# One bias table instead of 128 copies, four product banks, and the compression's small networks as steps of their own, in a two-layer attention trunk

## The chip, the cores and the metric

The kernel runs on one core of a Trainium2 chip. The metric is the time of one execution on the device, in microseconds (us); lower is better. Engines are named as the profile names them: PE multiplies matrices (PEld loads its stationary operand), DVE is VectorE, ACT is ScalarE, POOL is GpSimd, and SP issues DMAs.

## What is computed

A trunk of two layers over 256 tokens of width 1024, float32 in and out. The part of the reference that the change touches, cut:

```python
for i in range(DEPTH):                                # 2
    h = h + 0.5 * swiglu(rms_norm(h, g[i, 0]), ffn1_wi[i], ffn1_wo[i])
    n = rms_norm(h, g[i, 1])
    ... = split_cols(n @ w_in[i], IN_SPLITS)
    ya = diff_attention(..., bias_a)                  # 4 heads
    yb = nsa_attention(..., bias_b, cmp_pos, cmp_w1, cmp_w2)   # 8 heads, 2 groups
    yc = swa_sink_attention(..., bias_c)              # 8 heads, window 128
    h = h + (sig(ga) * (ya @ w_br[0]) + sig(gb) * (yb @ w_br[1]) + sig(gc) * (yc @ w_br[2])) @ w_out[i]
    h = h + 0.5 * swiglu(...)                         # second ffn
    h = h + sigmoid(rms_norm(h, g[i, 3]) @ w_ple_gate[i]) * (p[i] @ w_ple[i])
# a head's bias depends on the distance alone: table[rel_bucket(qpos - kpos)]
# in nsa_attention, beside attention over all keys (twice):
k_cmp = gelu(blocks(kc) @ w1[0]) @ w2[0]              # 15 compressed keys, also v_cmp
p_c = masked_softmax(q k_cmp + bias(dist_c));  o_c = p_c @ v_cmp
```

## The kernel before

**Products.** Every large product (`product`, L290) has the activations as stationary operand (128 tokens by 128 features) and 512 weight columns as moving operand, for two token tiles `t`. Float32 is carried as two parts, so that each step `k` is three matmuls (`mul3`, L219: L220, L221, L222). Token tile 1 runs `skew` steps behind tile 0. The result of each tile takes a PSUM bank of the tag `mm`, of which there are two (`mm_bank`, L191). Two more banks have the tag `s` (attention scores), three `tp` (transposes) and one `y`.

**Weights.** `load` (L257) brings 512 KB at a time into one of four `raw` buffers through SP's queue; ACT (L213) and DVE (L208) split it into `wh` and `wl`, in six buffers each. `fetch` keeps three pieces ahead of the use, in the order of the stream. A compile-time planner with a timing model orders each engine's instructions; each engine's queue then runs in that order.

**Feed-forward.** `ffn` (L437) runs 11 products `ff` of 256 gate and 256 up columns, evacuated by ACT L458 (`act`) and DVE L459 (`gated`), turned by DMA transposes on SP's queue (L427), and then two products `fo`.

**Bias.** In the first feed-forward of layer 0, `setup` (L1041) runs in four pieces, after products 4, 5 and 8 and between the two `fo` products. It makes a table of 20 heads by 384 distances (`tb`), writes it to DRAM (`table`, L1061) and from there 128 times into a second DRAM tensor, `rev` (L1062). `rev_band` (L1033) reads a tile `band` of four heads from `rev`, each partition from an address one element lower than the one above it, so that column and partition give the distance. Two bands are read in `setup` on POOL's queue (for `cbias`, L1086 and L1087), ten later on SP's queue.

**Attention.** `attention` (L488) runs the projections A0, A1, A2, Ck, Cq, Bk, Bv, Bq, the three `branch` parts (a gate product and a `br` product for each half of the columns) and the two `wo` products. Between the steps `k` of a product, `Flow.tick` (L162) advances one generator, the side: `attend_a` (L581) from Ck on, `attend_c` (L864) from Bv on, `attend_b` (L793) from `compress` on, at 0.75, 0.6 and 0.7 steps per tick. `flow.join` runs what is left of a side at one place: of A after Bk (L962), of C after branch 0 (L969), of B within branch 1 (L941). The bias is added by DVE L529, which also takes the minimum.

**Compression.** `compress` (L685) runs 64 matmuls `cmp` of 256 columns and then, in one piece, the rest of the two small networks: `c_sb` (L709), eight matmuls `gl` (L712), the gelu on ACT and DVE, `hid`, the matmuls `kc` (L726) and `vc` (L738). `attend_cmp` (L761) computes the scores `sc` against the compressed keys, their softmax `pc` for eight heads of 16 columns, and turns it by eight transposes `pct` (L787) per token tile, one for each head, into 16-row operands `pcT` [16, 2, 512]. `second` (L827) multiplies them with `vc` (16 rows) at L843, as the last part of `yb`. It calls `attend_cmp` before the first use of each token tile, and until `kc` is there it waits with empty steps.

Of the kernel before, what the change touches and what calls it, by code (L numbers as in the profile page):

```python
# [33 lines left out]
PACE_A, PACE_B, PACE_C = 0.75, 0.7, 0.6  # L34
# [101 lines left out]
def _constants():  # L136
    u = np.arange(REV)
    dist = 255 - u
# [10 lines left out]
    return {"onehot": onehot, "dead": dead, "cmask": cmask, "ident": np.eye(128, dtype=np.float32),  # L149
# [3 lines left out]
class Flow:  # L153


    def __init__(self):
        self.side, self.pace, self.due = None, 0.0, 0.0

    def start(self, side, pace):
        self.side, self.pace, self.due = side, pace, 0.0  # L160

    def tick(self):  # L162
        if self.side is not None:
            self.due += self.pace
            while self.due >= 1.0:
                self.due -= 1.0
                if next(self.side, self) is self:
                    self.side = None
                    return

    def join(self):
        if self.side is not None:
            for _ in self.side:
                pass
            self.side = None
# [3 lines left out]
def trunk(ctx: ExitStack, tc: tile.TileContext, a: dict, out: bass.AP, index: list):  # L179
# [11 lines left out]
    def mm_bank(name):  # L191
        return bank("mm", 2, name)

# [294 lines left out]
    def attention(i, norm, after):  # L488
# [3 lines left out]
        def begin():  # L492
            nonlocal pool
            pool = phase("attn")
            for t in range(NT):
                merged[t] = pool.tile([128, D], F32, name=f"merged{t}")
# [58 lines left out]
        def band(first):  # L555
            b = pool.tile([128, 4, 256], F32, tag="band", bufs=2, name="band")
            rev_band(b, first)
# [23 lines left out]
        def attend_a():  # L581
            bnd = band(0)

            def first(u):
# [6 lines left out]
                for st in softmax([p[:, j, :nk] for j in range(4)], [s[j // 2][:, j % 2, :nk] for j in range(4)],  # L591
                                  [bnd[:, 2 * m + j % 2, 256 - nk:] for j in range(4)]):
# [90 lines left out]
        kc, vc = [None], [None]  # L683

        def compress():  # L685
# [22 lines left out]
            c_sb = stage()  # L708
            nc.vector.tensor_copy(c_sb[:64], c_ps[:64])  # L709
            g_ps = tp_bank("gl")[:, :128]  # L710
            for k in range(4):
                nc.tensor.matmul(g_ps[:, 32 * k:32 * k + 32], c_sb[:64, 128 * k:128 * k + 128], fold, start=True, stop=True)  # L712
# [6 lines left out]
            nc.vector.tensor_tensor(gl, gl, g_ps, op=ALU.mult)  # L719
            hid = pool.tile([128, 2, 128], F32R, name="hid")  # L720
            split(hid[:, 0], hid[:, 1], gl)
            w2h, w2l = w2(0)
# [10 lines left out]
            split(kt[:, 0], kt[:, 1], kbd)  # L733
            v_ps = tp_bank("vc")
            for g in range(2):
                for f in range(2):
                    s, n = slice(256 + 64 * f, 320 + 64 * f), slice(64 + 32 * f + 16 * g, 80 + 32 * f + 16 * g)
                    mul3(v_ps[:16, 64 * g:64 * g + 64], hid[:, 0, n], hid[:, 1, n], w2h[:, s], w2l[:, s], f == 0, f == 1)  # L738
            vc[0] = pool.tile([16, 2, 128], F32R, name="vc")
            values(vc[0], v_ps[:16, :128], None)  # L740
# [20 lines left out]
        def attend_cmp(t):  # L761
# [20 lines left out]
            for g in range(2):  # L782
                ps = tp_bank("pct")
                for par in range(2):
                    for m in range(2):
                        j = 2 * par + m
                        nc.tensor.transpose(ps[:16, 128 * j:128 * j + 128], p[:, 4 * g + 2 * m + par, :], ident)  # L787
                T = pool.tile([16, 2, 512], F32R, tag="pcT", bufs=2, name="pcT")
                split(T[:, 0], T[:, 1], ps[:16])
                pcT[t, g] = T  # L790
                yield

        def attend_b():  # L793
# [33 lines left out]
            def second(u, p):  # L827
                g, t, ss = u
                if yB[t] is None:
                    while kc[0] is None:  # L830
                        yield
# [340 lines left out]
```

## Time and profile before

| | us |
|---|---|
| median of 3 runs | 1372.09 |
| lowest, highest | 1371.64, 1373.06 |
| profiled execution | 1372.78 |
| its span, first to last instruction | 1371.0 |

The profiled execution takes 1.78 us more than its span (what lies before the first and after the last instruction), and 0.69 us more than the median. Its trace has a record of each instruction on each engine, of DMA packets, and of the share of PE's clock that was granted (1.00 is 2.4 GHz, 0.50 is 1.2 GHz). In a row `x8` is a count; in square brackets or after a bar stands the time the engine was idle before the instruction, and what ended that idle time.

### The profile page before, as it was taken

What the parts mean: (1) busy time and instruction counts of PE and PEld (TensorE: products, weight loads), DVE (VectorE), ACT (ScalarE), POOL (GpSimd) and SP (SyncE); (2) the same over time, 40 slices, a digit from 0 to 9 for tenths busy, and PEclk for the clock granted to TensorE, in tenths of its full rate; (3) what the DMA queues carried; (4) which work ended last, traced back from release to release, by engine and by line L of the source; (5) the groups of instructions that cost most, each with busy time, mean ns of one, the idle gap of its engine ahead of it and who ended that gap; (6) DMA issues with size and microseconds to landing.
All of it is one profiled execution on the core that took longest, in us unless ns stands there. A gap on an engine that the chain in (4) does not pass through costs nothing.

```text
span 1371.0 us, 18293 instructions
## 1 busy us (share of the span) xinstructions
PE 1341.5 (98%) x6454; PEld 1098.2 (80%) x6454; DVE 944.7 (69%) x1779; ACT 779.4 (57%) x1378; POOL 19.0 (1%) x37
## 2 busy tenths in 40 slices
PE   8988999999999999999999999999999999999997
PEld 6766888887787788888888888888887778888886
DVE  7546656777886766766677665667697776776665
ACT  7435445668766455545665444566785656455454
POOL 0000000000000000000000000000000000000000
PEclk9999999999999999999999999999999999999999
DMA  8797757444653467775657885754547435777662
GB/s 306 199 265 227 216 177 237 142 152 156 215 175 109 153 189 213 215 210 192 203 189 219 223 226 171 235 170 137 162 151 232 127 122 168 216 222 218 194 202 84
DMA packets 121993, 261.07 MB, mean 190 GB/s; under 512 B 56816, under 2 KB 62372, under 8 KB 121774
## 3 DMA queue, kind: packets, MB, share of 16 engines
q1 hardware_dynamic: 121006, 254.34, 60.3%
q0 software_dynamic: 464, 5.01, 1.2%
q8 instruction: 50, 0.82, 0.2%
q10 hardware_dynamic: 432, 0.56, 0.1%
q14 instruction: 41, 0.34, 0.1%
HBM read 247.26 MB, written 5.01 MB: 184 GB/s over the span
## 4 chain that ended last, share of the span: by engine, by line
PE 88%; DMA 5%; DVE 3%; ACT 2%; issue 1%; SPq 0%; POOLq 0%; POOL 0%; DVEq 0%; ACTq 0%
PE ff L220 10%; PE ff L221 10%; PE ff L222 10%; PE fo L221 6%; PE fo L220 6%; PE fo L222 6%; DMA raw<-in_wst 4%; PE gate L220 3%; PE gate L221 3%; PE gate L222 3%; PE s L520 2%; PE A L220 2%; PE A L222 2%; PE A L221 2%; PE br L220 2%; PE br L222 2%
## 5 line engine op out<-in xcount | busy, mean ns | idle before, releaser
L208 DVE TENSOR_TENSOR wl<-raw,wh 128x1024 fp32r<-128x1024 f32 (+1 forms) x450 | 540.8, 1211 | 176.2 <-ACT wh L213 169.5
L213 ACT ACTIVATE wh<-raw 128x1024 fp32r<-128x1024 f32 (+1 forms) x450 | 469.4, 1049 | 227.7 <-PE fo L222 85.8
L220 PE MATMUL ff<-wh,nT 128*128 128x512 f32 x704 | 276.8, 395 | 13.0 <-DVE gated L459 8.4
L221 PE MATMUL ff<-wl,nT 128*128 128x512 f32 x704 | 276.2, 393 | 0.7 <-DVE wl L208 0.5
L222 PE MATMUL ff<-wh,nT 128*128 128x512 f32 x704 | 275.0, 391 | 0.0
L220 PEld LDWEIGHTS ff<-wh,nT 128*128 128x128 f32 x704 | 133.2, 189 | 45.6 <-DVE gated L459 11.0
L221 PEld LDWEIGHTS ff<-wl,nT 128*128 128x128 f32 x704 | 133.3, 189 | 30.0 <-DVE wl L208 2.7
L222 PEld LDWEIGHTS ff<-wh,nT 128*128 128x128 f32 x704 | 133.3, 189 | 27.9
L221 PE MATMUL fo<-wl,gT 128*128 128x512 f32 x352 | 134.2, 392 | 0.0
L222 PE MATMUL fo<-wh,gT 128*128 128x512 f32 x352 | 133.7, 389 | 0.0
L220 PE MATMUL fo<-wh,gT 128*128 128x512 f32 x352 | 133.2, 390 | 0.0
L458 ACT ACTIVATE act<-ff,stats 128x256 f32<-128x256 f32 x88 | 41.4, 473 | 104.0 <-PE ff L222 103.9
L459 DVE TENSOR_TENSOR gated<-act,ff 128x256 f32<-128x256 f32 x88 | 36.6, 417 | 74.3 <-ACT act L458 74.3
L221 PE MATMUL gate<-wl,nT 128*128 128x512 f32 x192 | 77.5, 404 | 1.5 <-DVE wl L208 1.5
L220 PE MATMUL gate<-wh,nT 128*128 128x512 f32 x192 | 78.8, 410 | 0.0
L222 PE MATMUL gate<-wh,nT 128*128 128x512 f32 x192 | 77.3, 402 | 0.0
L220 PEld LDWEIGHTS fo<-wh,gT 128*128 128x128 f32 x352 | 66.1, 188 | 13.9
L222 PEld LDWEIGHTS fo<-wh,gT 128*128 128x128 f32 x352 | 66.1, 188 | 13.4
L221 PEld LDWEIGHTS fo<-wl,gT 128*128 128x128 f32 x352 | 66.1, 188 | 13.3
L213 ACT ACTIVATE gT<-whole 128x512 fp32r<-128x512 f32 (+1 forms) x48 | 28.3, 590 | 63.0 <-DVE whole L432 62.2
L531 ACT ACTIVATE p<-p,st 128x128 f32<-128x128 f32 (+1 forms) x128 | 56.8, 447 | 12.2 <-DVE st L529 12.0
L320 ACT ACTIVATE nT<-nt,ngt 128x128 fp32r<-128x128 f32 x112 | 32.0, 369 | 30.8 <-PE nt L228 30.8
(297 smaller groups left out, 2002.8 us busy)
## 6 DMA issues: line engine op xcount, KB each, us to landing
raw<-in_wst SPq DMA_DIRECT2D x438, 512.0 KB, 4.4
band<-rev SPq DMA_DIRECT2D x10, 512.0 KB, 4.1
rev<-table POOLq DMA_DIRECT2D x1, 3840.0 KB, 18.3
raw<-in_wbv SPq DMA_DIRECT2D x4, 420.0 KB, 3.0
flip<-cut SPq DMA_TRANSPOSE x96, 3.8
xt<-in_xt SPq DMA_DIRECT2D x4, 256.0 KB, 5.3
raw<-in_wst SPq DMA_DIRECT2D x4, 256.0 KB, 4.0
h<-in_x SPq DMA_DIRECT2D x2, 512.0 KB, 8.0
```

What stands on the lines that cost most here:

```text
L208: nc.vector.tensor_tensor(o, x, y, op=ALU.subtract)
L213: nc.scalar.activation(hi, src, AF.Copy)
L220: nc.tensor.matmul(ps, xh, wh, start=start, stop=False)
L221: nc.tensor.matmul(ps, xh, wl, start=False, stop=False)
L222: nc.tensor.matmul(ps, xl, wh, start=False, stop=stop)
L320: ins = nc.scalar.activation(T[:, 0, k + m, :], src[:, 128 * m:128 * m + 128], AF.Copy, scale=ngt[:, self.row, k + m:k + m + 1])
L458: nc.scalar.activation(act, ps[:, :256], AF.Silu, scale=norm.r(t))
L459: nc.vector.tensor_tensor(held[t][:, 256 * (f % 2):256 * (f % 2) + 256], act, ps[:, 256:], op=ALU.mult)
L520: nc.tensor.matmul(o, q[r, x, qb[m], t * 128:(t + 1) * 128], kk, start=x + y == 0, stop=x == 1)
L531: nc.scalar.activation(p[j], p[j], AF.Exp, bias=st[:, j:j + 1], scale=-1.0, accum_out=st[:, n + j:n + j + 1])
```

## The change

- The tensor `rev` and the DMA that fills it are gone. The table is stored by rising distance, bands are read from `table` itself with one element more per partition, and the users read a band's columns from right to left (`back`: a step of -1, for `cbias` of -16).
- `product` takes banks in turn from `mm` and `s`, two of each, outside the attention's projections and branches (`wide`).
- `Flow` has lanes, each a queue of sides. A, C and B follow each other in lane 0 (B at 0.75); a join waits for one side, and stands later: for A within branch 0, for C within branch 2.
- `compress` ends with the copy `c_sb`. The rest is the generator `compressed`, eleven steps in lane 1, one per tick, beside branch 2. The second weights are loaded by a step of their own before it.
- The compressed probabilities of all eight heads (128 columns) are turned by one transpose into `pcT` [128, 128]; for each group, `own` multiplies it with a mask of the group's heads into 128 rows by 4 x 128 and splits that. The values are copied to 128 rows (`rows_`), so that `vc` has 128 rows. `attend_cmp` is called at the end of `second`, where `pcT` is used.

```diff
-PACE_A, PACE_B, PACE_C = 0.75, 0.7, 0.6
+PACE_A, PACE_B, PACE_C = 0.75, 0.75, 0.6
...
-    dist = 255 - u
+    dist = u - 127
...
+    def step(self, lane):
+        if next(lane[0][0][0], self) is self:
+            lane[0].pop(0)
 
     def tick(self):
...
+        for lane in self.lanes.values():
+            if lane[0]:
+                lane[1] += lane[0][0][1]
+                while lane[1] >= 1.0 and lane[0]:
+                    lane[1] -= 1.0
+                    self.step(lane)
...
+    def product_bank(name):
+
+        wide[1] += 1
+        return bank("s" if wide[0] and wide[1] % 4 >= 2 else "mm", 2, name)
...
-                            ps[t] = mm_bank(f"{name}{t}")
+                            ps[t] = product_bank(f"{name}{t}")
...
+            c_sb[0] = pool.tile([128, 512], F32, name="c_sb")
+            nc.vector.tensor_copy(c_sb[0][:64], c_ps[:64])
+
+        def compressed():
...
+            rows_ = base.tile([128, 2, 2, 128], F32R, tag="stage", bufs=4, name="rows")
+            for f in range(2):
+                for x in range(2):
+                    nc.vector.tensor_copy(
+                        rows_[:, x, f].rearrange("p (g h n) -> p g h n", g=2, h=4),
...
+                mul3(v_ps[:, :64], rows_[:, 0, f], rows_[:, 1, f], w2h[:, s], w2l[:, s], f == 0, f == 1)
...
-            for g in range(2):
-                ps = tp_bank("pct")
-                for par in range(2):
-                    for m in range(2):
-                        j = 2 * par + m
-                        nc.tensor.transpose(ps[:16, 128 * j:128 * j + 128], p[:, 4 * g + 2 * m + par, :], ident)
-                T = pool.tile([16, 2, 512], F32R, tag="pcT", bufs=2, name="pcT")
-                split(T[:, 0], T[:, 1], ps[:16])
-                pcT[t, g] = T
-                yield
+            ps = tp_bank("pct")
+            transposes(ps, [p.rearrange("p h n -> p (h n)")])
+            pcT[t] = pool.tile([128, 128], F32, tag="pcT", bufs=2, name="pcT")
+            nc.scalar.activation(pcT[t], ps[:, :128], AF.Copy)
+            yield
+
+        def own(t, g):
+
+            o = stage("own").rearrange("p (j q) -> p j q", j=4)
+            nc.vector.tensor_tensor(o, pcT[t][:, None, :].to_broadcast([128, 4, 128]),
+                                    hmask[:, 4 * g:4 * g + 4, None].to_broadcast([128, 4, 128]), op=ALU.mult)
+            T = pool.tile([128, 2, 4, 128], F32R, tag="pT", bufs=3, name="pcT")
+            split(T[:, 0], T[:, 1], o)
+            return T
...
                 if ss[-1] == 1:
-                    weighted(y_ps[g, t], vc[0][:, g], pcT[t, g], False, True)
+                    if t not in pcT:
+                        while kc[0] is None:
+                            yield
+                        yield from attend_cmp(t)
+                    T = own(t, g)
+                    yield
+                    weighted(y_ps[g, t], vc[0][:, 0], T.rearrange("p x j q -> p x (j q)"), False, True)
...
-        yield flow.join
-        yield lambda: flow.start(attend_c(), PACE_C)
+        yield lambda: start("c", attend_c(), PACE_C)
...
+        yield second_weights
+        yield lambda: start("b", attend_b(), PACE_B)
         w1 = streamed(i, "w1", 256)
-        w2 = Weights(384, [(a["w2"][i], 384)], 1)
         yield compress
-        yield from branch(2, yC)
-        yield from branch(1, yB, True)
+        yield lambda: start("compressed", compressed(), 1.0, 1)
+        yield from branch(2, yC, "c")
+        yield from branch(1, yB, "b", True)
+        yield lambda: wide.__setitem__(0, True)
...
+        queue.dma_start(b, bass.AP(tensor=ap.tensor, offset=ap.offset + first * REV, ap=[[1, 128], [REV, 4], [1, 256]]))
+
+    def back(b, n, step=1):
+
+        return bass.AP(tensor=b.tensor, offset=b.offset + step * (n - 1), ap=list(b.ap)[:-1] + [[-step, n]])
...
-        nc.gpsimd.dma_start(rev, table.to_broadcast([128, NB * REV]))
```

## Rows read from the trace of the kernel before

**Rows 1.** The page: busy time of the engines (share of the span, instructions), and the chain of work that ended last, by engine.

```profile
PE 1341.5 (98%) x6454; PEld 1098.2 (80%) x6454; DVE 944.7 (69%) x1779; ACT 779.4 (57%) x1378; POOL 19.0 (1%) x37
...
PE 88%; DMA 5%; DVE 3%; ACT 2%; issue 1%; SPq 0%; POOLq 0%; POOL 0%; DVEq 0%; ACTq 0%
```

**Rows 2.** Busy time in two stretches of 32 us in the first feed-forward of layer 0: from:to, length, busy time and instructions of PE, PEld, DVE, ACT and POOL, granted clock, DMA share, GB/s.

```profile
87.00:119.00 32.00, 22.55 (x79) 15.97 (x78) 18.91 (x25) 14.26 (x17) 1.54 (x2) 0.89 0.94 265
130.00:162.00 32.00, 32.00 (x143) 26.50 (x142) 19.33 (x31) 14.70 (x18) 0.00 (x0) 1.00 0.74 206
```

**Rows 3.** Timeline of POOL (start, duration, what; idle time before and its end).

```profile
69.25 0.72 POOL L1061 DMA_DIRECT2D table<-tb  x1 [51.94 <-DVE nlam L1074]
71.47 0.56 POOL L1062 DMA_DIRECT2D rev<-table  x1 [1.51 <-DMA table<-tb]
90.04 1.54 POOL L1035 DMA_DIRECT2D band<-rev  x2 [18.00 <-DMA rev<-table]
```

**Rows 4.** DMA issues of the whole span: size of each, median us from issue to landing.

```profile
band<-rev SPq DMA_DIRECT2D x10, 512.0 KB, 4.1
rev<-table POOLq DMA_DIRECT2D x1, 3840.0 KB, 18.3
...
band<-rev POOLq DMA_DIRECT2D x2, 512.0 KB, 9.7
```

**Rows 5.** Timeline of PE, two matmuls with a wait before them.

```profile
32.91 0.80 PE L220 MATMUL ff<-wh,nT 128*128 128x512 f32 x1 [2.40 <-DVE gated L459]
...
113.94 0.50 PE L220 MATMUL ff<-wh,nT 128*128 128x512 f32 x1 [3.18 <-DVE gated L459]
```

**Rows 6.** Timeline of ACT and of DVE at the same place, before 33 us.

```profile
31.17 0.82 ACT L458 ACTIVATE act<-ff,stats 128x256 f32<-128x256 f32 x2
...
30.06 2.47 DVE L208 TENSOR_TENSOR wl<-raw,wh 128x1024 fp32r<-128x1024 f32 x2 [0.70 <-ACT wh L213]
32.44 0.75 DVE L459 TENSOR_TENSOR gated<-act,ff 128x256 f32<-128x256 f32 x2
```

**Rows 7.** Busy time in stretches with a fallen clock and around them (columns as in rows 2).

```profile
408.00:411.80 3.80, 3.80 (x29) 2.88 (x28) 3.79 (x9) 0.81 (x3) 0.00 (x0) 0.99 0.25 98
411.80:415.20 3.40, 3.40 (x9) 2.72 (x9) 2.76 (x14) 2.56 (x10) 0.00 (x0) 0.50 0.49 154
...
1032.50:1036.40 3.90, 2.94 (x17) 2.24 (x16) 3.87 (x9) 3.06 (x4) 0.00 (x0) 1.00 0.60 221
1036.40:1039.80 3.40, 3.40 (x10) 2.61 (x9) 2.74 (x5) 0.56 (x3) 0.00 (x0) 0.50 0.86 254
...
1080.80:1084.20 3.40, 3.40 (x9) 2.67 (x8) 2.76 (x16) 2.47 (x10) 0.00 (x0) 0.50 0.47 158
...
32.90:36.30 3.40, 3.39 (x8) 2.71 (x9) 2.77 (x6) 0.04 (x1) 0.00 (x0) 0.50 1.02 313
```

**Rows 8.** Timeline of PE in the first of these stretches (operand sizes: rows*columns of the stationary operand, then the moving one).

```profile
408.01 0.85 PE L520 MATMUL s<-kB,qB 64*128 64x256 f32 x9
...
409.56 0.39 PE L746 MATMUL yb<-pcT,vc 16*128 16x512 f32 x1
409.88 0.28 PE L220 MATMUL sc<-kc,qB 128*128 128x32 f32 x1
```

**Rows 9.** Groups of PE instructions (busy us, mean ns | idle time before them in all, and what ended it), both layers.

```profile
L228 PE MATMUL pt<-ident,p 128*128 128x128 f32 x168 | 26.6, 275 | 1.6 <-DVE half L655 1.6
...
L712 PE MATMUL gl<-fold,stage 64*128 64x32 f32 x16 | 2.1, 275 | 1.8 <-DVE stage L709 1.8
```

**Rows 10.** Timeline of PE, and of DVE, at the end of `compress` in layer 0.

```profile
364.71 0.50 PE L221 MATMUL gate<-wl,nT 128*128 128x512 f32 x1 [0.77 <-DVE wl L208]
...
367.33 1.07 PE L712 MATMUL gl<-fold,stage 64*128 64x32 f32 x8 [0.83 <-DVE stage L709]
...
368.67 0.40 PE L221 MATMUL gate<-wl,nT 128*128 128x512 f32 x1
...
367.20 4.61 DVE L208 TENSOR_TENSOR wl<-raw,wh 128x1024 fp32r<-128x1024 f32 x4
```

**Rows 11.** The chain in order of time: the transposes `pct` of one token tile.

```profile
396.96 0.87 PE pct L787 x8
```

**Rows 12.** Groups of DVE and then of ACT instructions, shapes kept apart.

```profile
L208 DVE TENSOR_TENSOR pT<-pt,pT 128x512 fp32r<-128x512 f32 x36 | 23.7, 684 | 0.5
L529 DVE CUSTOM_DVE_ANT_0 p<-s,band 128x256 f32<-128x256 f32 x48 | 17.6, 419 | 7.9 <-PE pt L228 7.9
...
L208 DVE TENSOR_TENSOR pcT<-pct,pcT 16x512 fp32r<-16x512 f32 x8 | 5.1, 672 | 0.1
...
L779 DVE TENSOR_TENSOR pc<-pc,st 128x128 f32<-128x128 f32 x4 | 1.2, 292 | 0.1
...
L1087 DVE COPY cbias<-band 128x30 f32<-128x30 f32 x4 | 0.7, 180 | 0.0
...
L1086 DVE COPY cbias<-band 128x14 f32<-128x14 f32 x4 | 0.7, 166 | 0.0
...
L213 ACT ACTIVATE pT<-pt 128x512 fp32r<-128x512 f32 x36 | 20.2, 591 | 19.1 <-PE pt L228 19.0
```

**Rows 13.** Busy time in the attention of layer 0, from C's projections to the last branch (columns as in rows 2), and its part from the end of `compress` on.

```profile
250.00:456.00 206.00, 203.20 (x1128) 165.63 (x1126) 160.69 (x398) 138.16 (x319) 2.78 (x4) 0.99 0.49 157
...
370.00:456.00 86.00, 85.82 (x441) 68.50 (x440) 66.17 (x145) 50.18 (x100) 0.00 (x0) 0.98 0.49 158
```

More of the change, by code (lines that the diff above doesn't have):

```diff
@@ L148, in _constants @@
     cmask = ((128 * t + ql - 16 * m - 31 >= 0) & (m < 15)).astype(np.float32).reshape(128, 32)
-    return {"onehot": onehot, "dead": dead, "cmask": cmask, "ident": np.eye(128, dtype=np.float32),
+    own = np.arange(8)[:, None] == np.array([4 * g + 2 * pr + par for g in range(2) for par in range(2) for pr in range(2)])
+    hmask = own.repeat(16, 0).astype(np.float32)
+    return {"onehot": onehot, "dead": dead, "cmask": cmask, "hmask": hmask, "ident": np.eye(128, dtype=np.float32),
             "fold": np.tile(np.eye(32, dtype=np.float32), (2, 1))}
@@ L156, in __init__, with start, join @@
     def __init__(self):
-        self.side, self.pace, self.due = None, 0.0, 0.0
-    def start(self, side, pace):
-        self.side, self.pace, self.due = side, pace, 0.0
-    def tick(self):
[L163 to L175, printed above, removed]
+        self.lanes = {}
+    def start(self, side, pace, lane=0):
+        self.lanes.setdefault(lane, [[], 0.0])[0].append((side, pace))
+        return side
+    def step(self, lane):
+        if next(lane[0][0][0], self) is self:
+            lane[0].pop(0)
+    def tick(self):
+        for lane in self.lanes.values():
[4 more added lines that the diff above has]
+                    self.step(lane)
+    def join(self, side):
+        while any(s is side for lane in self.lanes.values() for s, _ in lane[0]):
+            for lane in self.lanes.values():
+                if lane[0]:
+                    self.step(lane)
 @with_exitstack
@@ L556, in band @@
             b = pool.tile([128, 4, 256], F32, tag="band", bufs=2, name="band")
[L557 removed]
+            read_band(b, first)
             return b
@@ L591, in first @@
                 for st in softmax([p[:, j, :nk] for j in range(4)], [s[j // 2][:, j % 2, :nk] for j in range(4)],
-                                  [bnd[:, 2 * m + j % 2, 256 - nk:] for j in range(4)]):
+                                  [back(bnd[:, 2 * m + j % 2], nk) for j in range(4)]):
                     yield
@@ L682, in attention, with second_weights @@
         w1 = w2 = None
-        kc, vc = [None], [None]
+        def second_weights():
+            nonlocal w2
+            raw = base.tile([128, SUB], F32, tag="raw", bufs=RAWS, name="w2raw")
+            nc.sync.dma_start(raw[:, :384], a["w2"][i])
+            w2 = pool.tile([128, 2, 384], F32R, name="w2")
+            split(w2[:, 0], w2[:, 1], raw[:, :384])
+        kc, vc, c_sb = [None], [None], [None]
         def compress():
@@ L805, in first @@
                     sr = [s[j // 2].rearrange("p m (k n) -> p m k n", k=2)[:, j % 2, k] for j, k in rows]
-                    br = [bnd[g][:, j, 128:] for j, k in rows]
+                    br = [back(bnd[g][:, j], 128) for j, k in rows]
                 else:
@@ L811, in first @@
                     sr = [s[j // 2][:, j % 2] for j in range(4)]
-                    br = [bnd[g][:, j] for j in range(4)]
+                    br = [back(bnd[g][:, j], 256) for j in range(4)]
                 n = len(pr)
@@ L879, in first @@
                 st = None
-                for st in softmax(pr, [s[j // 2][:, j % 2, :nk] for j in range(4)], [bnd[g][:, j, 256 - nk:] for j in range(4)], sink):
+                for st in softmax(pr, [s[j // 2][:, j % 2, :nk] for j in range(4)], [back(bnd[g][:, j], nk) for j in range(4)], sink):
                     yield
@@ L902, in attend_c, with branch @@
             yield from pipelined([(g, t) for g in range(2) for t in range(NT)], first, second)
-        def branch(b, yT, last=False):
+        def branch(b, yT, side, last=False):
             def parts(c):
```

59 lines of the change are left out of this document (33 added, 26 removed).

## Prediction

> **What bounds the kernel now.** First the shares of the engines and the chain [rows 1]: PE is busy for 1341.5 of 1371.0 us, and 88% of the chain is PE. So time is gained in three ways only: fewer PE instructions, PE's idle time, and stretches in which PE is busy but slow. DVE at 69% matters where it makes PE wait. Then stretch by stage: in a settled stretch of the first feed-forward PE issues 143 matmuls in 32 us, 0.224 us each; in the stretch just before it, 79 in the same 32 us [rows 2]. The 64 missing ones are 64 x 0.224 = 14.3 us, the largest loss in the trace. POOL's timeline says what happens there [rows 3]: the copy into `rev` is issued at 71.5 us, and the two bands that wait for it at 90.0. The issue table has its size [rows 4]: 3840 KB, 18.3 us, while DMA runs at a share of 0.94 [rows 2]. PE's timeline at the end of this stretch shows a wait of 3.18 us for `gated`, that is for a PSUM bank [rows 5]. The same wait, 2.40 us, stands at 32.91 us. Last, the clock: there are stretches in which PE was granted 0.50 of its clock, 1.2 GHz in place of 2.4; PE is busy all through them and issues 8 to 10 matmuls where 3.4 us would hold 15 [rows 7].
>
> **No copy into `rev`.** It takes away 3.84 MB of writes and one wait of POOL. The two bands go right behind the table, near 71.5 us in place of 90.0, and 1 MB of them is still read beside the weights; they took 9.7 us to land, while the copy's effects were still there [rows 4]. What comes late next is a weight piece behind them. At 0.74 in the settled stretch [rows 2], DMA has a quarter of its time free, and three pieces are fetched ahead, so I leave 1.0 us for it, with 0 and 6 as ends (6 is about the 9.7 us less the 4.1 that a band takes on SP's queue [rows 4]). Gain 14.3 - 1.0 = **13.3**, ends 8.3 and 14.3.
>
> **Bands read from `table`.** As many reads of as many pieces, out of 30 KB in place of 3.84 MB. The nearest row is the copy itself, which read the same 30 KB 128 times in 18.3 us, 210 KB per us, with the weights beside it [rows 4]; that is well above what a band needs (512 KB in 4.1 us are 125 KB per us). Cost 0; the upper end is a rival below.
>
> **Bands read backwards.** No row has a negative step. The nearest are the copies into `cbias` with a step of 16: 30 elements take 180 ns, 14 take 166 [rows 12], 0.9 ns per element. Contiguous elements taken in the other order are nearer to the plain read than that. Cost 0; again a rival has the other end.
>
> **Four banks.** In the copy's stretch they gain nothing of their own beyond the 14.3 already counted. At the start of the kernel PE waited at 32.91 us for a bank. ACT had put `act` behind `wh` pieces and ran it at 31.17; DVE ran `gated` at 32.44, behind two `wl` that end at 32.5 [rows 6]. With two more banks the next product needs weights only, and the pieces that it starts with had been split by then, as DVE was on later ones. That takes away 2.40 us and the fall of the clock after it: 8 matmuls in 3.4 us where 15.2 fit, 7.2 x 0.224 = 1.6 [rows 7]. Of 4.0 I take **3.5**, since weights may be late by some of it; ends 0 and 4.0. In settled feed-forward PE has no idle time [rows 2], and the banks bring nothing.
>
> **Lanes and later joins.** Counted from the code, A has 42 steps, and 48 ticks at 0.75 give 36 before its join; the rest was run in one piece behind Bk. There the transposes `pt` wait 1.6 us in both layers together for DVE's `half` [rows 9]. Spread over Bv this goes: **1.5**, ends 0 and 1.6. C starts 8 ticks later and still ends within branch 0, so its moved join finds nothing to do.
>
> **The small networks as steps.** `gl` waits 1.8 us for the copy `c_sb` in both layers [rows 9]. Most of this is no gain: the `gate` matmul behind it needs a `wl` from a DVE group that begins at 367.20 and takes 4.61 us for four, so the first is there at about 368.4, and `gate` runs at 368.67 [rows 10]. What goes is 0.2 us per layer, **0.4**, ends 0 and 1.8. The wait for `wl` of 0.77 us before it [rows 10] stays, as the 64 `cmp` matmuls still use up weights faster than they come. In layer 1 a fall of the clock follows this place (10 matmuls in 3.4 us, 5.2 x 0.224 = 1.2 lost) after a stretch with PE busy for 2.94 of 3.90 us [rows 7]. Half of it: **0.7**, ends 0 and 1.2.
>
> **One transpose for eight.** 32 transposes in all become 4. Eight take 0.87 us [rows 11], 0.109 each: 28 x 0.109 = **3.0**, all on PE, ends 2.5 and 3.05.
>
> **128-row operands.** The matmuls with `vc` have as many columns as before, so their own time stays. The clock: at 411.8 us it falls to 0.50 although PE was busy for 3.80 of 3.80 us [rows 7]. In these 3.8 us PE ran scores of 64 rows, `yb` of 16 rows and `sc` of 32 columns [rows 8], work that fills little of the array. The fall at 1080.8 is the same place of layer 1. Each loses 6.2 x 0.224 = 1.4. With 128 rows, and with `own` between `sc` and `yb`, this work no longer stands in one block; I take **2.0** of 2.8, ends 0 and 2.8.
>
> **What it adds.** PE: `vc` becomes 12 matmuls with 128 stationary columns in place of 24 with 16, at most 12 x 0.109 = 1.3, less what they took: **-0.5**, ends -1.3 and 0. DVE per layer: four masks of 128x512 at 0.684 (the row of `pT` with that shape), four splits at 0.684 in place of four at 0.672, four copies of 128x128 at 0.29 [rows 12]: 2.74 + 0.05 + 1.16 = 3.95 us. DVE has 206.0 - 160.7 = 45.3 us idle in this attention, 19.8 of them behind `compress` [rows 13], which hide most of it; **-1.0** for both layers, ends -7.9 and 0. ACT changes by two copies per layer.
>
> **The end of B.** B has 72 steps before and 74 after, and waits for `kc` with 8 empty steps before and 15 after, since `kc` is ready 11 ticks later. 112 ticks give 78 steps at 0.7 and 84 at 0.75: two or three steps were left for its join, and five or six will be. Behind them stand the last `yb`, `gather` and the `br` products of token tile 1. A mask, a split on ACT and one on DVE in a row are 0.68 + 0.59 + 0.68 = 1.95 us [rows 12]; the `br` products of token tile 0 can cover part. **-1.4** for both layers, ends -3.9 and 0.
>
> **The sum.** 13.3 + 3.5 + 1.5 + 0.4 + 0.7 + 3.0 + 2.0 = 24.4 gained, 0.5 + 1.0 + 1.4 = 2.9 lost: 21.5 net. The profiled execution took 1372.78 us: 1351.3 after. It lay 0.7 above the median of the runs, so the forecast is **1350.6**. By the ends, all at their best give 29.0, all at their worst nearly nothing; not all go the same way, and three quarters of these spreads together, without the costs of the rivals, reach from 1343 to 1356.
>
> **Rivals.**
> *The early bands still starve PE, and the banks do not help.* The two POOL bands come while SP's DMA transposes and weights compete as before, and the planner, whose timing model orders ACT and DVE, puts evacuations and splits in another unlucky order. For it: the wait at 113.94 came 24 us after the bands were issued [rows 3, 5]. Against it: the 18.3 us of copy are gone. Price 5.0 + 3.5: 1359. Chance 0.15.
> *The clock still falls in both attentions.* `sc` with 32 columns and the scores with 64 rows are still there [rows 8]. It gives back 2.0 + 0.7: 1353.3. Chance 0.17. The Trainium skill ("TensorE: Matmul & The Clock Gate", section "Why this matters for your kernels") names idle gaps between bursts of matmuls as what drops PE to the lower clock. By that rule the rows of an operand would not matter, and the sum would be smaller by the 2.0. The trace does not agree here: no idle time stands before the fall at 411.8 [rows 7].
> *The table is a hot spot.* All 128 partitions read within a few KB at once. If a band takes twice its 4.1 us [rows 4], ten reads on SP's queue stand 41 us longer ahead of weights; with DMA at 0.49 in attention [rows 13] half is hidden: 20.5 lost, 1371. The copy's 210 KB per us speaks against it. Chance 0.05. The Trainium skill ("DMA: Bandwidth & Descriptors", section "Latency and other measured facts") has partition rows at a pitch of 4 MiB at half the rate of a pitch of 512 KiB, and suspects that streams in step meet in the same memory channel. If that held for a pitch of one element, a band would take about 8.2 us, as priced above; the trace has no read of this form.
> *Slower: the backward read.* Place: the 128 instructions L529, 64 x 256 + 64 x 128 = 24,576 elements per partition. Each added ns per element is 24.6 us of DVE, 12.3 per layer, against 45.3 idle [rows 13], of which I count half as usable. With 3 ns added, 36.9 - 22.6 = 14.3 stand out per layer, 28.6 in all: 1379. It makes the change slower from about 2.7 ns per element on. Against it: 0.9 ns at a step of 16 [rows 12]. Chance 0.04.
>
> **How the numbers follow.** Forecast 0.57, starved 0.15, clock 0.17, hot table 0.05, slower 0.04, and 0.02 for better than all ends, where settled stretches gain as well. A measurement of this kernel can tell about 0.2% (2.7 us) from no change. Faster: 0.57 + 0.17 + 0.15 + 0.02 = 0.91. Same: the hot table, 0.05. Slower: 0.04. The range is 1340 to 1361: it holds the forecast, the clock and the starved case, and leaves out some 0.14.
>
> **What would show it.** Right: 143 matmuls or nearly so in every 32 us from 36 to 160, no wait of `ff` for `gated` in the first 120 us; 4 `pct`; `pt` without its wait for `half`; no granted clock of 0.50 where `yb` meets `pcT`. Wrong: weights that land late near 75 us, bands that take over 5 us, L529 over 419 ns at 128x256 [rows 12], idle time before `br` at the end of B, or DVE waits of PE within branch 2 larger than before.

## The result and the profile after

The changed kernel took **1361.03 us** (median of 4 runs, 1359.98 to 1362.90) against 1371.87 (1369.92 to 1373.06) before: a ratio of 0.9924, with a 95% interval from 0.9907 to 0.9941. It gained 10.8 us, half of the 21.5 forecast. The page has the span, then busy time, share of it and instructions:

```profile
span 1361.1 us, 18234 instructions
PE 1329.9 (98%) x6414; PEld 1096.7 (81%) x6414; DVE 947.3 (70%) x1795; ACT 781.9 (57%) x1382; POOL 18.8 (1%) x36
```

PE is busy for 11.6 us less than in [rows 1], but idle for 31.2 us in place of 29.5. So something was given back. The first stretch of [rows 2] again, then two with a fallen clock (columns as there):

```profile
87.00:119.00 32.00, 32.00 (x143) 26.50 (x142) 22.14 (x31) 16.09 (x21) 0.00 (x0) 1.00 0.77 239
68.60:72.00 3.40, 3.40 (x9) 2.65 (x9) 3.40 (x5) 2.20 (x3) 0.00 (x0) 0.50 0.77 227
450.90:454.30 3.40, 3.40 (x11) 2.69 (x10) 2.25 (x4) 1.11 (x3) 0.00 (x0) 0.50 0.68 235
```

That stretch holds 143 matmuls in place of 79, and no `ff` waits for `gated` in the first 120 us. The clock was at 0.50 from 945.8 to 949.2 and from 1099.4 to 1106.2 us as well. POOL's timeline and the issue table answer to [rows 3, 4]:

```profile
80.05 0.71 POOL L1121 DMA_DIRECT2D table<-tb  x1 [62.76 <-DVE tb L1120]
84.62 1.83 POOL L1091 DMA_DIRECT2D band<-table  x2 [3.87 <-DMA table<-tb]
```

```profile
band<-table SPq DMA_DIRECT2D x10, 512.0 KB, 4.6
...
band<-table POOLq DMA_DIRECT2D x2, 512.0 KB, 6.1
```

The bands land 4.6 us after their issue (4.1 before), those on POOL's queue after 6.1 (9.7); that is far from twice as long, and the table is no hot spot. The Trainium skill ("DMA: Bandwidth & Descriptors", section "Latency and other measured facts") has rows at some pitches at half the rate of others; at this pitch of one element the trace shows no halving.

What stays of the early loss is a wait at 68 us. PE's timeline, then DVE's ahead of it (start, us; in brackets the idle time before it and what ended it):

```profile
68.08 0.50 PE L236 MATMUL ff<-wl,nT 128*128 128x512 f32 x1 [2.41 <-DVE wl L223]
```

```profile
54.17 0.17 DVE L1123 TENSOR_SCALAR nsink<-nsink 128x16 f32<-128x16 f32 x1 [3.97 <-DMA nsink<-in_sinks]
...
61.26 0.43 DVE L1127 TENSOR_TENSOR lprod<-lamp 128x256 f32<-128x256 f32 x1 [1.20 <-DMA lamp<-in_lamp]
...
66.82 1.21 DVE L223 TENSOR_TENSOR wl<-raw,wh 128x1024 fp32r<-128x1024 f32 x1
```

DVE stood for 3.97 and 1.20 us behind small loads of setup and came late to the `wl` for which PE waited; whether the loads cause the wait, e4 and e14 ask below. The clock then fell (second window).

The larger loss is at the end of B. PE's timeline in layer 0:

```profile
418.40 0.39 PE L237 MATMUL gate<-wh,nT 128*128 128x512 f32 x1
...
421.61 0.26 PE L237 MATMUL sc<-kc,qB 128*128 128x32 f32 x1
...
428.35 0.33 PE L243 MATMUL pct<-ident,pc 128*128 128x128 f32 x1 [3.17 <-DVE pc L821]
...
430.43 0.51 PE L786 MATMUL yb<-pcT,vc 128*128 128x512 f32 x1 [0.44 <-ACT pcT L228]
431.16 0.50 PE L787 MATMUL yb<-pcT,vc 128*128 128x512 f32 x1 [0.22 <-DVE pcT L223]
...
433.50 0.47 PE L786 MATMUL yb<-pT,vB 128*128 128x512 f32 x1 [0.48 <-DVE yt L796]
...
449.67 0.87 PE L243 MATMUL mt<-ident,merged 128*128 128x128 f32 x6 [2.75 <-DVE merged L968]
```

The last matmul of `gate` is issued at 418.40, the last `sc` of token tile 1 at 421.61, and `pct`, which needs the softmax of this `sc`, at 428.35, after 3.17 us of idle PE. The waits shown from 428.35 on are 7.1 us; layer 1 has 3.16 at `pct` too. Before, `sc` of this tile began at 409.88 [rows 8] (here at 418.98), although all work of the layer was then some 15 us later by the copy's loss. DVE between `sc` and `pct`:

```profile
422.24 0.28 DVE L810 TENSOR_TENSOR pc<-sc,cbias 128x128 f32<-128x128 f32 x1
...
424.77 0.69 DVE L967 SCALAR_TENSOR_TENSOR th<-th,br 128x512 f32<-128x512 f32 x1 [0.35 <-PE br L237]
425.49 0.69 DVE L968 TENSOR_TENSOR merged<-merged,th 128x512 f32<-128x512 f32 x1
...
428.00 0.29 DVE L821 TENSOR_TENSOR pc<-pc,cmask 128x128 f32<-128x128 f32 x1
```

The steps of `pc` queue between those of `p` and of `merged`: from the last `sc` to `pct` it is 6.7 us, and PE had 14 matmuls for this time. Last, the group of DVE that answers to L529 in [rows 12], and `pt` of [rows 9]:

```profile
L545 DVE CUSTOM_DVE_ANT_0 p<-s,band 128x256 f32<-128x256 f32 x48 | 17.4, 419 | 0.0
```

```profile
L243 PE MATMUL pt<-ident,p 128*128 128x128 f32 x168 | 27.2, 288 | 2.2 <-DVE half L671 2.1
```

The backward read of a band costs nothing: 419 ns for 128x256, as forward (L529 there). The wait of `pt` for `half` has not gone; it is 2.1 us, and was 1.6.

### The profile page after: what moved, and what is told of

Read it like the earlier page. It is cut to its first block, busy times and chain, and to the rows that moved or that the text cites. A ratio compares the mean times of both kernels' runs of the same rounds, so it can differ in the third digit from the quotient of the medians.

```text
span 1361.1 us, 18234 instructions
## 1 busy us (share of the span) xinstructions
PE 1329.9 (98%) x6414; PEld 1096.7 (81%) x6414; DVE 947.3 (70%) x1795; ACT 781.9 (57%) x1382; POOL 18.8 (1%) x36
## 4 chain that ended last, share of the span: by engine, by line
PE 83%; DVE 7%; ACT 3%; DMA 3%; issue 2%; SPq 0%; POOLq 0%; POOL 0%; DVEq 0%; ACTq 0%
PE ff L236 10%; PE ff L235 10%; PE ff L237 10%; PE fo L236 6%; PE fo L235 6%; PE fo L237 6%; DVE wl L223 3%; PE gate L235 3%; PE gate L236 3%; PE gate L237 2%; PE A L237 2%; PE A L236 2%; PE A L235 2%; PE s L536 1%; DMA flip<-cut 1%
## 5 line engine op out<-in xcount | busy, mean ns | idle before, releaser
L237 PE MATMUL ff<-wh,nT 128*128 128x512 f32 x704 | 274.3, 391 | 0.0
L235 PE MATMUL ff<-wh,nT 128*128 128x512 f32 x704 | 271.7, 392 | 0.1
L235 PE MATMUL gate<-wh,nT 128*128 128x512 f32 x192 | 77.1, 402 | 1.3 <-DVE merged L965 1.1
L237 PEld LDWEIGHTS fo<-wh,gT 128*128 128x128 f32 x352 | 66.1, 188 | 13.3
L236 PEld LDWEIGHTS fo<-wl,gT 128*128 128x128 f32 x352 | 66.1, 188 | 13.3
L237 PE MATMUL gate<-wh,nT 128*128 128x512 f32 x192 | 75.3, 394 | 0.0
L447 DVE COPY whole<-flip 128x512 uint16<-128x512 uint16 (+1 forms) x96 | 38.0, 432 | 15.2 <-DMA flip<-cut 14.8
```

The lines of the kernel that those rows point to most:

```text
L235: nc.tensor.matmul(ps, xh, wh, start=start, stop=False)
L236: nc.tensor.matmul(ps, xh, wl, start=False, stop=False)
L237: nc.tensor.matmul(ps, xl, wh, start=False, stop=stop)
L447: tc.keep_in_program_order(nc.vector.tensor_copy(halves(whole)[:, :128 * m, w], flip[:, w, :m].rearrange("p a b -> p (a b)")))
```

## Experiments

Times are medians in us; each has the ratio to the kernel before that ran with it, with its 95% interval. The kernel before took 1370.8 to 1373.7 beside them, so 3 us or less between runs that were not taken together show nothing by themselves. Theory at the start: the late `attend_cmp` loses what the rest gains.

**Where attend_cmp stands.** In the changed kernel it runs when its result is first multiplied; in e1, as before, ahead of a token tile's first `yb`:

```diff
                 if yB[t] is None:
+                    while kc[0] is None:
+                        yield
                     yB[t] = y_tile("yB")
+                    yield from attend_cmp(t)
...
-                    if t not in pcT:
-                        while kc[0] is None:
-                            yield
-                        yield from attend_cmp(t)
```

> The changed kernel with one move: attend_cmp is called before the first use of each token tile, as in the kernel before, and not at the end of second. The masks and splits of own stay, so DVE does the same work. Theory 1 (late chain): in the changed kernel PE waits at the end of B for the softmax of the second token tile (3.17 and 3.16 us for pc, and what follows it); started earlier, this is hidden, and the time falls from 1361 by 4 to 9 us, to 1352 to 1357. Theory 2 (too much DVE work, 3.95 us more per layer by own and the copies): the waits stay in other places, 1360 to 1362.

1352.64 us, 0.984 (0.9823 to 0.9857): 8.4 us less than the changed kernel. PE's timeline: the last `sc` of token tile 1 begins at 392.3, and `pct` has no idle time before it. Then the stretch from the last `cmp` matmul to the last `wo` in both layers, first in the changed kernel, then in e1 (columns as in [rows 2]).

```profile
392.30 0.26 PE L237 MATMUL sc<-kc,qB 128*128 128x32 f32 x1
407.78 0.27 PE L243 MATMUL pct<-ident,pc 128*128 128x128 f32 x1
```

```profile
349.94:472.85 122.91, 114.54 (x562) 92.86 (x562) 93.65 (x197) 70.55 (x133) 0.00 (x0) 0.99 0.46 153
1021.91:1142.96 121.05, 115.29 (x562) 93.90 (x562) 93.80 (x198) 70.91 (x133) 0.56 (x1) 0.97 0.48 157
```

```profile
347.93:465.60 117.67, 114.93 (x570) 93.15 (x570) 94.61 (x196) 72.29 (x134) 0.55 (x1) 1.00 0.48 159
1013.82:1131.88 118.06, 114.96 (x571) 93.15 (x570) 94.48 (x196) 71.38 (x132) 0.55 (x1) 1.00 0.48 157
```

The two stretches are 8.2 us shorter in e1, and PE is idle in them for 5.8 us in place of 14.1: the loss lies where theory 1 has it.

e2 moves token tile 1 alone forward, at its first unit:

```diff
                     yB[t] = y_tile("yB")
+                    if t == 1:
+                        yield from attend_cmp(t)
```

> The changed kernel with attend_cmp moved for token tile 1 only, to the beginning of second of its first unit; for token tile 0 it stays at the end. Theory 1 (late chain): as the waits stand before pct of token tile 1 alone, this does as much as the move for both or more, since B has fewer empty steps before kc is there: 1351 to 1356. Theory 2 (DVE work): 1360 to 1362.

1357.05, 0.9873 (0.9854 to 0.9892): about half of e1's gain, just outside the expected range. `pct` no longer waits, but `pt` waits for `p`, 1.9 us in both layers. e3 hurries B instead:

```diff
-PACE_A, PACE_B, PACE_C = 0.75, 0.75, 0.6
+PACE_A, PACE_B, PACE_C = 0.75, 1.0, 0.6
```

> The changed kernel with B at 1.0 steps per tick in place of 0.75; attend_cmp stays where the change put it. B then ends some 15 to 20 ticks earlier. Theory 1 (late chain): the end of B is covered by the gate products of branch 1, the waits for pc shrink, and the time falls by 3 to 8 us, to 1353 to 1358. Theory 2 (DVE work): the same work in fewer ticks makes DVE later than now, 1361 to 1366.

1363.94, 0.9929 (0.9904 to 0.9954): a miss. `sc` came 4 us earlier (417.3) and `pct` waited 3.23 us all the same. A faster pace does not help.

**Setup's small loads.** e4 moves the work on `nsink`, `lam` and `sg` behind the issue of the bands:

```diff
-        nc.vector.tensor_scalar(nsink, nsink, -1.0, None, op0=ALU.mult)
...
         yield
         bands = []
...
             bands.append(b.rearrange("p (par pr) c -> p par pr c", par=2))
+        nc.vector.tensor_scalar(nsink, nsink, -1.0, None, op0=ALU.mult)
...
         yield
```

> The changed kernel with the small DVE and ACT instructions of setup that wait for nsink, subln and lamp moved from its second piece to its third, some 30 us later; their loads stay where they are. Theory 3 (DVE's queue stands still behind small loads: 3.97 us for nsink and 1.20 for lamp before the wait of PE at 68 us): the wait of 2.41 us for wl and the fall of the clock after it go, 1361 falls by 3 to 5 us, to 1356 to 1358. Rival (DMA is the limit there, at a share of 0.98 to 1.32 between 58 and 66 us): the wait stays, 1360 to 1362.

1361.31, 0.9904 (0.9886 to 0.9921). The wait at 67 us was 1.41 in place of 2.41. The clock did not fall there, but it fell at 271.7, where it had not, and no clear gain is left. e9 has this edit on e1:

> The changed kernel with attend_cmp ahead of a token tile's first use (as in e1) and with the work on nsink, lam and sg one piece of setup later (as in e4). Theory, both losses are separate and each edit takes its own away: e1's 1352.6 less the 2.6 us that the wait and the fall of the clock at 68 us cost beyond e4: 1350, from 1348 to 1352. Rival, the loss at 68 us only moves to a later place, as part of it did in e4: 1352 to 1354.

1351.98, 0.9858 (0.984 to 0.9876): the same as e1 within the intervals. The two ranges meet here, so it does not decide between them.

**Table and banks.** e5 is the kernel before with `table` in place of `rev`, e6 with the four banks alone, e10 with both:

```diff
-            rev_band(b, first)
+            read_band(b, first)
...
-        nc.gpsimd.dma_start(rev, table.to_broadcast([128, NB * REV]))
```

```diff
-                            ps[t] = mm_bank(f"{name}{t}")
+                            ps[t] = product_bank(f"{name}{t}")
```

> The kernel before with one part of the change: no copy into rev, bands read from table, backwards. The prediction's term (13.3) gives 1358 to 1360. Rival (part of that stretch is lost to the two POOL bands and to waits for a PSUM bank, which only the four banks take away): 1362 to 1366. If the backward read or the small table cost anything, L529 takes over 419 ns at 128x256, or a band over 5 us to land.

1358.66, 0.9916 (0.9894 to 0.9937): as the prediction's term has it.

> The kernel before with one part of the change: products take banks in turn from mm and s outside attention's projections and branches. The prediction's term (3.5, the wait at 32.9 us and the clock after it) gives 1368 to 1369. Rival (in the stretch with the copy into rev, too, PE stood still for banks and not for weights, 5.0 us of its idle time): 1361 to 1366, and then the two parts do not add up in the changed kernel.

1357.18, 0.9909 (0.9882 to 0.9937): a miss, and the most telling one. The copy is still there. Its place on POOL, its issue, the weights issued beside it (86 to 105 us) and the window of [rows 2] in e6:

```profile
86.75 0.56 POOL L1071 DMA_DIRECT2D rev<-table  x1 [3.38 <-DMA table<-tb]
```

```profile
rev<-table POOLq DMA_DIRECT2D x1, 3840.0 KB, 18.1
raw<-in_wst SPq DMA_DIRECT2D x4, 512.0 KB, 14.1
```

```profile
87.00:119.00 32.00, 32.00 (x142) 26.48 (x142) 18.82 (x29) 14.90 (x19) 1.84 (x3) 1.00 1.05 323
```

PE issues 142 matmuls, one less than undisturbed, beside a copy of 18.1 us and a DMA share of 1.05. In the kernel before, the weights issued beside the copy (71 to 92 us), ACT and PE show what the copy did there:

```profile
raw<-in_wst SPq DMA_DIRECT2D x3, 512.0 KB, 17.5
```

```profile
89.96 2.24 ACT L213 ACTIVATE wh<-raw 128x1024 fp32r<-128x1024 f32 x2 [8.90 <-DMA raw<-in_wst]
...
91.07 1.22 PE L220 MATMUL ff<-wh,nT 128*128 128x512 f32 x2 [3.37 <-ACT wh L213]
```

Weights came late beside the copy in both kernels (17.5 and 14.1 us; 4.4 over the whole trace before). Before, PE waited for them too: of its 9.4 us of idle time from 87 to 119, 4.5 are waits for `wh` and `wl` and 5.0 for `gated`, that is for a bank. In e6 it waited for neither there. But the copy in e6 also starts 15 us later, 86.75 against 71.47 [rows 3], and no run has four banks with the copy at its old place. So that four banks are enough for this kernel is shown; that it is the banks and not the place of the copy is argued.

> The kernel before with one table and with four banks, and nothing else. Theory, the two take away the same loss (PE's stall beside the copy) and only 15 us are there to gain: 1371.7 - 15.1 = 1356.6, from 1355 to 1358, with PE's wait near 68 us still there. Rival, each has a gain of its own, as the runs with one of them alone would add up: 1371.7 - 13.1 - 14.6 = 1344. The prediction's terms, 13.3 + 3.5: 1354.9.

1357.97, 0.9903 (0.9884 to 0.9921). Alone, table and banks gain 13.1 and 14.6; together 12.8. They take away one and the same loss. The bank wait at 32.91 us [rows 5] is gone in e10, but PE waits for `wh` and `wl` at 68 us instead, 2.60 and 0.93.

**128 rows.** e7 is the kernel before with one transpose, `own` and 128-row `vc`, and `attend_cmp` where it was:

```diff
-                    weighted(y_ps[g, t], vc[0][:, g], pcT[t, g], False, True)
+                    T = own(t, g)
+                    yield
+                    weighted(y_ps[g, t], vc[0][:, 0], T.rearrange("p x j q -> p x (j q)"), False, True)
```

> The kernel before with one part of the change: one transpose of the compressed probabilities per token tile, masks and splits of own, vc in 128 rows; attend_cmp stays before the first use, the joins and compress stay. The prediction's terms (3.0 for transposes, 2.0 for the clock, less 0.5 and 1.0) give 3.5 less, 1368, and no granted clock of 0.50 in the two places where yb meets pcT. Theory 2 (DVE work of own): 1371 to 1375. Theory 1 (only the late call hurts): 1367 to 1369.

1366.76, 0.9968 (0.9954 to 0.9981): 5.0 gained, and the clock does not fall where `yb` meets `pcT`. e8 is the changed kernel without table and banks:

```diff
-            read_band(b, first)
+            rev_band(b, first)
...
-    wide = [True, 0]
+    wide = [False, 0]
```

> The changed kernel without the table and without the four banks: the copy into rev and forward reads are back, products take mm only. What is left are the attention edits: lanes, later joins, networks as steps, 128-row operands, the late call of attend_cmp. The prediction's terms for these come to 4.7 less than before, 1367. Theory 1 (the late chain costs 6 to 8 us in both layers, more than the rest of the attention edits bring): 1372 to 1377.

1375.19, 1.0037 (1.0019 to 1.0055): the attention's edits together are a loss of 3.4 us. e11 is e10 with e7's edit, and no lanes, later joins or steps:

> The kernel before with one table, four banks and 128-row operands, attend_cmp where it was; no lanes, no later joins, no small networks as steps. It differs from e1 (1352.6) by these alone. By the prediction's terms for them (1.5 + 0.4 + 0.7) it should be 2.6 us slower than e1: 1355. Theory, they bring nothing, since PE still waited for half and the wait for wl hid the copy c_sb: 1351 to 1353.5, no slower than e1.

**1348.51, 0.983 (0.9813 to 0.9847): the best of all**, 9.5 us under e10, which ran beside it. Not all of this is e7's edit: of the 11.7 us between the two traces, 7.3 lie from the last `cmp` to the last `wo` of both layers, and 4.0 before the attention of layer 0, where this edit adds only one small load (PE waits at 67 us for 1.70 in place of 3.53, and the clock does not fall). Both windows where `yb` meets `pcT` and `sc`, in e10 and then in e11:

```profile
394.00:397.80 3.80, 3.80 (x29) 2.67 (x27) 3.80 (x9) 1.23 (x3) 0.00 (x0) 0.99 0.33 125
397.80:401.20 3.40, 3.40 (x11) 2.61 (x11) 3.13 (x14) 2.15 (x8) 0.00 (x0) 0.51 0.50 154
```

```profile
390.00:394.00 4.00, 4.00 (x27) 3.24 (x26) 4.00 (x10) 1.99 (x4) 0.00 (x0) 1.00 0.75 244
400.00:404.00 4.00, 4.00 (x19) 3.30 (x18) 3.89 (x12) 2.92 (x5) 0.00 (x0) 1.00 0.13 20
```

With 16-row operands the clock falls, as in [rows 7], with PE busy throughout; with e7's edit it does not. The same holds in all traces: before, e5, e6 and e10 have this fall in both layers, the other kernels in neither. The edit brings 128 rows, one transpose and `own` between `yb` and `sc` together; which of the three it is was not tried.

**Joins, steps, and what makes B late.** e12 is e1 with the joins of A and C where they were:

```diff
+        yield lambda: flow.join(sides["a"])
         yield lambda: start("c", attend_c(), PACE_C)
...
+        yield lambda: flow.join(sides["c"])
         yield second_weights
```

> The kernel of e1 with the joins of A and C where they were before (A behind Bk and ahead of C, C behind branch 0); lanes and steps stay. By the prediction's term for the later joins it should be 1.5 us slower than e1: 1354, with a longer wait of pt for half. Theory, the later joins bring nothing: within 0.8 us of e1, 1352 to 1353.4, and the wait of pt for half as long as in e1.

1351.17, 0.985 (0.9832 to 0.9867); `pt` waits 1.7 us, less than with later joins. The later joins bring nothing, and e11, without any of this, is 2.7 us faster than e12 beside it. e13 puts the late `attend_cmp` (the removed lines of e1's diff) into e11:

> The kernel of e11 (one table, four banks, 128-row operands, no lanes, joins and steps as before) with attend_cmp moved to the end of second, as in the changed kernel. Theory, the late attend_cmp costs by itself: about the 8.4 us between the changed kernel and e1, 1355 to 1359, with PE waits of about 3 us for pct in both layers. Rival, it costs only together with the lanes and steps, which make kc ready later: within 2 us of e11, 1347 to 1351, and no wait for pct over 1 us.

1349.91, 0.9851 (0.9824 to 0.9878). **The theory fell here**: late `attend_cmp` alone costs next to nothing, so a second edit must be in it. e14 is e11 with e4's edit:

> The kernel of e11 with the work on nsink, lam and sg one piece of setup later, as in e4 and e9. Theory, e9 gained nothing on e1 (1352.0 and 1352.6), so the wait at 68 us is given back by weights that are late elsewhere: 1347 to 1350. Rival, without the lanes the wait and its fall of the clock go for good: 1345 to 1347.

1349.22, 0.9839 (0.9813 to 0.9864), no gain: the wait is still there, 2.36 us at 69.2 against 1.70 at 66.9 in e11, and the clock falls at it. So the small loads are not what the wait hangs on. For the second edit, e15 is the changed kernel with e12's joins, e16 has the small networks in one piece, and e17 has both:

```diff
-        yield lambda: start("compressed", compressed(), 1.0, 1)
+        yield lambda: list(compressed())
```

> The changed kernel (late attend_cmp, lanes, steps) with the joins of A and C where they were before. Theory, the small networks as steps make kc late, and the joins are no part of it: about as the changed kernel, 1358 to 1362, with PE waits of about 3 us for pct in both layers. Rival, the later joins push B's work back: 1350 to 1354 and no wait for pct over 1.5 us.

1358.46, 0.9909 (0.9878 to 0.994); `pct` waits 2.92 us in layer 0.

> The changed kernel with the small networks run in one piece behind compress in place of steps in a lane; the late attend_cmp and the later joins stay. Theory, kc is ready earlier, B is some 6 us earlier against the gate products, and these cover the chain from sc to yb: 1350 to 1354, the waits for pct below 1.5 us. Rival, the steps are no part of it: 1358 to 1362, with the waits for pct as in the changed kernel.

1361.12, 0.9927 (0.9902 to 0.9951); `pct` waits 3.22 us.

> The changed kernel with both edits of e15 and e16: the joins where they were, and the small networks in one piece behind compress. The late attend_cmp stays, and so do PACE_B 0.75 and w2 in a tile of its own, which e13 does not have. Theory, the later joins and the steps each put B far enough back, so that undoing one alone did not help: as e13, 1348 to 1353, with waits for pct below 1.5 us. Rival, neither is it, but PACE_B or the early w2: 1357 to 1361, with waits for pct of 3 us as in e15 and e16.

1359.58, 0.9901 (0.9882 to 0.9921); `pct` waits 2.39 us. Neither joins nor steps are the second edit. e18 is e13 with one more edit, `w2` loaded and split ahead of B:

```diff
+        yield second_weights
         yield lambda: flow.start(attend_b(), PACE_B)
         w1 = streamed(i, "w1", 256)
-        w2 = Weights(384, [(a["w2"][i], 384)], 1)
```

> The kernel of e13 (late attend_cmp, no lanes, joins and steps as before, PACE_B 0.7) with w2 loaded and split ahead of B into a tile of its own, as in the changed kernel, in place of one more piece of the weight queue. Theory, the early w2 moves the weight pieces by one place, the splits of hid come behind more wl on DVE's queue, kc misses the gap between gate and br, and B gets late: 1356 to 1361, with a wait for pct over 2 us. Rival, it is PACE_B 0.75 that e17 has and e13 has not: within 2 us of e13, 1348 to 1352, no wait for pct over 1.2 us.

1360.74, 0.9921 (0.9891 to 0.9951): the whole loss is back, 10.8 us, of which 9.9 lie from the last `cmp` to the last `wo` of both layers. DVE in e13, and then in e18, from the first `gl` to `hid`:

```profile
350.38 2.34 DVE L217 TENSOR_TENSOR wl<-raw,wh 128x1024 fp32r<-128x1024 f32 x2
352.65 0.21 DVE L725 TENSOR_SCALAR gl<-gl 128x128 f32<-128x128 f32 x1
...
359.27 0.28 DVE L217 TENSOR_TENSOR hid<-gl,hid 128x128 fp32r<-128x128 f32 x1
```

```profile
351.22 4.62 DVE L217 TENSOR_TENSOR wl<-raw,wh 128x1024 fp32r<-128x1024 f32 x4
355.76 0.21 DVE L733 TENSOR_SCALAR gl<-gl 128x128 f32<-128x128 f32 x1
...
362.38 0.28 DVE L217 TENSOR_TENSOR hid<-gl,hid 128x128 fp32r<-128x128 f32 x1
```

Four `wl` stand between the matmuls `gl` and DVE's first `gl` in place of two, and `hid` is done 3.1 us later. ACT's first `gl` is late too, 354.32 against 351.15: one more `wh` is ahead of it, and that had waited 1.14 us for its weights. PE in e13 and in e18:

```profile
360.96 0.26 PE L231 MATMUL kc<-hid,wl 128*128 128x32 f32 x1
...
410.36 0.26 PE L231 MATMUL sc<-kc,qB 128*128 128x32 f32 x1
...
421.25 0.27 PE L237 MATMUL pct<-ident,pc 128*128 128x128 f32 x1
```

```profile
361.45 0.28 PE L229 MATMUL kc<-hid,w 128*128 128x32 f32 x1 [1.19 <-ACT hid L222]
...
367.28 0.26 PE L231 MATMUL kc<-hid,w 128*128 128x32 f32 x1
...
416.77 0.26 PE L231 MATMUL sc<-kc,qB 128*128 128x32 f32 x1
...
427.06 0.33 PE L237 MATMUL pct<-ident,pc 128*128 128x128 f32 x1 [3.31 <-DVE pc L803]
```

3 us on ACT and DVE become 6 on PE, as the other `kc` matmuls come only behind the next `br` block, and `sc` of tile 1 is 6.4 us later too. From it to `pct` it is 10.9 us in e13 and 10.3 in e18. Behind this `sc` PE had 47 matmuls in e13, 10.7 us at 0.227, and 29 in e18, 6.6 us: the wait of 3.31 us makes up most of the rest.

## Why the prediction was wrong

The gain was 10.8 us in place of 21.5. e11 leaves out the lanes, the later joins, the steps, B's pace of 0.75, the early `w2` and the late `attend_cmp`, and gains 22.3. So the other edits, which the prediction has at 1.2 gained (1.5 + 0.4 + 0.7 - 1.4), cost 11.5. That e11 comes so near the forecast is partly luck: copy and banks had been put 4.0 too high, the transposes and rows 6.0 too low. It is luck, too, that the measured time is near the 1359 of the first rival: the banks' 3.5 did come to nothing, but the early bands starved nothing, with 143 matmuls in their stretch. The prediction's ends add up to 28.75 at best and -2.3 at worst; three quarters of these spreads reach from 1345 to 1368, not from 1343 to 1356.

`attend_cmp` and `w2`, by ratio:

| | `w2` a piece of the queue | `w2` ahead of B |
|---|---|---|
| `attend_cmp` early | 0.983 (e11) | 0.984 (e1), 0.985 (e12) |
| `attend_cmp` late | 0.985 (e13) | 0.992 (e18), 0.992 (the change) |

(e1, e12 and the change also have lanes, steps and B at 0.75. No run has the early `w2` with the early call and without lanes.)

- **The end of B** is the step that failed: -1.4, with -3.9 as its end, against 8.4 (the change less e1) or 10.8 (e18 less e13). It counted one mask and two splits in a row, 1.95 us. What stands in a row is `sc`, softmax, `pct`, `own` and `yb`, and from the last `sc` to the last `pc` alone it is 6.7 us (the change) to 10.2 (e18) among DVE's other work. This matters only where nothing is left on PE to cover it. The early `w2`, an edit that the prediction did not price at all, took away that cover. Why it changes the order of `wl` and `gl` was not tried; that one piece fewer stands in the weight queue is how the code reads.
- **Copy and banks**, 13.3 and 3.5: 12.8 together (e10). The table's term held (13.1 alone, e5). The banks' sentence, "nothing of their own beyond the 14.3", was right for the sum, but not that the copy alone is the cause: PE stood still for weights and for banks, and either edit alone takes the stall away (e5, e6). The banks' 3.5 came to nothing beside the table: the wait at 32.91 went, and one at 68 us came; e4, e9 and e14 move it and gain nothing.
- **One transpose, 128 rows** (3.0 + 2.0 - 0.5 - 1.0 = 3.5): too small. 5.0 alone (e7), 9.5 beside table and banks (e11 less e10), of which 7.3 by the traces lie where the edit is; some 1.7 of them are a fall of the clock at 1022.4 us, behind a wait of `gl` of 0.95, that e10 has and e11 with the same wait has not. The fall of the clock without idle time goes away with this edit, as forecast. The Trainium skill ("TensorE: Matmul & The Clock Gate", section "Why this matters for your kernels") names idle gaps as what drops the clock. The new falls at 68.6 and 450.9 do stand behind 2.41 and 2.75 us of idle PE, e10's at 397.8 behind 3.80 of 3.80 us busy; and in e1 the clock stayed at 1.00 behind an idle gap of 2.21 us at 67.6.
- **Later joins** (1.5) and **steps** (0.4 + 0.7): nothing. `pt` waited 2.1 in place of 1.6, and a `wl` of 1.2 us is right ahead of `half` on DVE with the old joins (286.25 us, before) and the new (271.08). `gl` no longer waits in the changed kernel, but `gate` behind `compress` waits 1.21 and 1.35 us for `wl` in place of 0.77 and 0.75.
- **Backward read, hot table**: 0, as forecast, by the rows above. **`own`** costs no visible time where `attend_cmp` is early.

## What to carry to other kernels

Before a step is moved to its last possible place, lay out its whole chain over all engines, with the queues in it, and count the matmuls that are left behind it: the cover must be longer than the chain. An edit can cost next to nothing alone (the late call, 1.4 us in e13) and 8 to 11 us beside another, so where undoing one of them explains the loss, put that one alone into the best version as well. Two edits that each remove the same wait don't add up, and an early wait that goes may return at the next resource.

## What the hardware showed that was not expected

Beside a DMA copy of 3840 KB within 18.1 us, at a DMA share of 1.05 and with weights that took 14.1 us to land, a PE with four PSUM banks lost one matmul in 143. With two banks, and the copy issued 15 us earlier in the stream, 64 were missing in the same window. The granted clock fell to 0.51 with PE busy for 3.80 of 3.80 us, on operands of 64 and 16 rows and 32 columns, and stayed at 1.00 at the same place with 128 rows and `own` in between. fp32 operands read backwards took 419 ns for 128x256, as forwards.
